# Hybrid decoder layer on one core: modulation sums packed into the first six merges, lighter paced steps, and two loads moved

## The chip, the cores and the metric

The kernel runs on one core of a Trainium2 chip. The metric is the device time of one execution in microseconds (us). TensorE (PE) multiplies matrices, VectorE (DVE) and ScalarE (ACT) work on tiles element by element, GpSimd (POOL) issues the indirect gathers and SyncE (SP) issues nearly all other DMAs. Each engine runs its own list of instructions strictly in order and waits on semaphores for the others.

## The reference, cut to what matters

Everything is float32; D = 2048, 512 tokens, 16384 experts, 16 chosen by each of 8 heads.

```python
mod = silu(c) @ w_ada + b_ada                  # 2048 -> 6 * 2048
sh1, sc1, g1, sh2, sc2, g2 = split(mod, 6)
h = rms_norm(x, norm1_w) * (1 + sc1) + sh1
q, k, v, f_logit, u, gate_s, gate_a = split(h @ w_in)
y_ssm  = half_glu(s5_mixer(u))
y_attn = fox_attention(q, k, v, f_logit)
merged = sigmoid(gate_s) * (y_ssm @ w_ssm_up) + sigmoid(gate_a) * (y_attn @ w_attn_up)
x = x + g1 * (merged @ w_out)
h2 = rms_norm(x, norm2_w) * (1 + sc2) + sh2
ids, ws = product_key_top16(h2)                # 8 heads x 16 experts for each token
a = gelu(einsum('td,ted->te', h2, expert_u[ids])) * ws
x = x + g2 * einsum('te,ted->td', a, expert_v[ids])
```

## The kernel before

A product in float32 is made of three matmuls on a high and a low part (`mm3`, lines 88 to 90). The parts of a weight come from `split`: ACT copies the high part (L94), DVE subtracts the low part (L95). Weights arrive in units of 512 KB (`wf`, issued at L100, three buffers; `whi` and `wlo` two each). In the merges and in `wout` a unit feeds 24 matmuls of 512 columns.

**The start** (0 to about 165 us) works out modulations 0 and 1 by rows on PE and DVE while it loads `w_ada`, and the setup of the S5 mixer beside it. The generator `vectors` loads `b_ada`, the norm weights and some small vectors to tiles `v`, and at its second `next` PE transposes them (L282, L286) and DVE copies them to `col1` and `col2`. Its order is written out by hand.

**The merges** (about 600 to 1098 us). `half_glu`, eight rounds of `merge` and `gates`, then `wout` (to about 1300 us) are ordered by the tile scheduler, not by hand. One round with its gates takes 11 weight units (1 of `w_ssm_up`, 2 of `w_attn_up`, 8 of `w_in`). Between rounds the kernel computes modulations 2 to 5 (`ada`): for each block of 512 columns it loads 16 tiles of 256 KB (`y`, L299), and DVE multiplies each by a column of `cond` and adds it to an accumulator (L302 for the first, L304 for the other 15). `end()` then adds over partitions with four small products against a column of ones on PE (L309, eight recorded matmuls) and DVE adds the bias (L311). There are 16 blocks. The accumulators and the `y` tiles share the pool `yp`: 28 buffers, of which the attention and S5 outputs hold 24 until the last merge. Two blocks are begun after each of the eight rounds, and the last two end after the loop.

**`wout`** makes the output projection in four quarters `q` of eight units. The input `x` is read again for the residual (`xl`, 16 small loads for each quarter, L1050, two buffers); at the end of a quarter DVE transposes a piece (L1073) and adds `g1` times the product to it (L1074), which frees the PSUM tile.

**The experts** (from about 1650 us) are ordered by hand. 320 tokens are computed densely against all experts on PE; the other 192 are gathered: `gathered` is a generator which yields after each step, first for 128 tokens (128 steps with `expert_u`, L1495, then 128 with `expert_v`, L1507), then for 64 tokens spread over 128 partitions (64 and 64), and after each group 12 light steps that scale by `g2` and add to `x2`: DVE makes diagonal tiles (`dg`, L1522), PE broadcasts them (L1526, into `A`), DVE multiplies (L1529), for the second group PE also sums the two halves (L1534), DVE adds (L1535). `pace(r)` is called at set places of the dense loops; it adds `r` to `owed` and runs one step for each whole unit. In the main loop (`value stage`, about 1895 to 3685 us) `expert_v` blocks `vf` (512 KB, L1569, three buffers) are loaded by `load_v`, split (L1577, L1580) and multiplied into 320 columns. After it stand 16 more `value` steps of 12 matmuls, each followed by one `step()`, and `finish`, which transposes the result (L1867) and stores it.

Of the kernel before, what the change touches and what calls it, by code (L numbers as in the profile page):

```python
# [7 lines left out]
F32 = mybir.dt.float32  # L8
# [9 lines left out]
P = 128  # L18
S = 512
# [18 lines left out]
VF = 3  # L38
# [11 lines left out]
NT = 6  # L50
ST = 1
S0 = 75
RS = (0, 1, 3, 4, 5, 6, 7)
SH = (0,) * 8 + (2,) * 8
TW = -(-TD // 32) * 32
# [8 lines left out]
class Builder:  # L64
# [227 lines left out]
    def ada(self, m, q, pool, bufs=None, tag="adaw"):  # L292

        nc = self.nc
        c0 = m * D + q * S
        acc = self.t(pool, [P, S], F32, "acc" if bufs else tag, bufs=1 if bufs else None)
        for i in range(KT):
            w = self.t(pool, [P, S], F32, tag, bufs=bufs)
            nc.sync.dma_start(w, self.wa[:, i, c0:c0 + S])  # L299
            col = self.cond[:, i:i + 1]  # L300
            if i == 0:
                nc.vector.tensor_scalar(acc, w, col, None, op0=ALU.mult)  # L302
            else:
                nc.vector.scalar_tensor_tensor(acc, w, col, acc, op0=ALU.mult, op1=ALU.add)  # L304

        def end():
            ps = self.t(self.ptp, [P, 4], F32, "tp")
            for c in range(4):
                nc.tensor.matmul(ps[:, c:c + 1], acc[:, c * P:(c + 1) * P], self.ones[:, 0:1], start=True, stop=True)  # L309
            s = slice(m * KT + q * 4, m * KT + q * 4 + 4)  # L310
            nc.vector.tensor_add(self.modc[:, s], ps, self.col1[:, s])  # L311

        return end
# [4 lines left out]
    def start(self, es, w_u):  # L318
# [155 lines left out]
        vectors = self.vectors(sp)  # L474
        next(vectors)
        s5 = self.s5_setup(first)
        for _ in range(S0):
            next(s5)
        next(vectors)
        nrm = norm()  # L480
        pend = iter(())
        shares = []
        for q in range(4):
            rows = [self.t(pu, [P, S], F32, "row", bufs=2) for _ in range(2)]
            accs = [None, None]
            for n in range(KT):
                m, i0 = 1 - n % 2, n // 2 * 2
                w = take("a", q, m, i0)
                for e in range(2):
                    i, src, col = i0 + e, w[:, e], self.cond[:, i0 + e:i0 + e + 1]  # L490
                    if i in PE_ROWS:
                        mm(rows[m][0:1, :], col, src, start=i == PE_ROWS[0], stop=False)
                        continue
                    if accs[m] is None:
                        accs[m] = self.t(self.apool, [P, S], F32, "a")
                        V.tensor_scalar(accs[m], src, col, None, op0=ALU.mult)
                    else:
                        V.scalar_tensor_tensor(accs[m], src, col, accs[m], op0=ALU.mult, op1=ALU.add)
                    for _ in range(ST):
                        next(s5, None)  # L500
                load()
                if q == 0:
                    if n >= NT:
                        next(nrm, None)
                else:
                    if n in RS:
                        next(pend, None)
                for _ in range(SH[n]):
                    while shares and not any(True for _ in [0] if next(shares[0], 0) is None):
                        shares.pop(0)  # L510
            for _ in pend:
                pass
            if q == 0:
                for _ in nrm:
                    pass
            pend = rest(q, accs, rows)
# [925 lines left out]
    def gathered(self, gp):  # L1442
# [44 lines left out]
        for gi, (n, _, w) in enumerate(groups):  # L1487
            if gi:
                hr = rows(0, gi)
                yield  # L1490
                yield
            av = self.t(gp, [P, n], F32, f"av{gi}")
            for s in range(n):
                g = q.pop(0)
                V.scalar_tensor_tensor(g, g, 1.0, hr, op0=ALU.mult, op1=ALU.mult, accum_out=av[:, s:s + 1])  # L1495
                used[0] += 1
                yield
            nc.scalar.activation(av, av, AF.Gelu)
            yield
            V.tensor_mul(av, av, w)  # L1500
            acc = self.t(gp, [P, D], F32, "big", bufs=1)
            for s in range(n):
                g = q.pop(0)
                if s == 0:
                    V.tensor_scalar(acc, g, av[:, 0:1], None, op0=ALU.mult)
                else:
                    V.scalar_tensor_tensor(acc, g, av[:, s:s + 1], acc, op0=ALU.mult, op1=ALU.add)  # L1507
                used[0] += 1
                yield

            m = NX if gi else P
            if gi:
                rsum = self.t(gp, [P, NX], F32, "rsum")
                V.tensor_copy(rsum, self.ident[:, 0:NX])
                for r in range(1, REP):
                    V.tensor_add(rsum, rsum, self.ident[:, r * NX:(r + 1) * NX])
            x2 = q.pop(0)
            for c4 in range(4):
                c = slice(c4 * S, (c4 + 1) * S)
                dg = self.t(self.up, [P, 4, P], F32, "ulo", bufs=4)  # L1520
                for i in range(4):
                    V.tensor_scalar(dg[:, i], self.ident, self.mcol(5, 4 * c4 + i), None, op0=ALU.mult)  # L1522
                yield
                ps = self.t(self.pA, [P, S], F32, "A", bufs=2)
                for i in range(4):
                    nc.tensor.matmul(ps[:, i * P:(i + 1) * P], self.ones, dg[:, i], start=True, stop=True)  # L1526
                if gi == 0:
                    yield
                V.tensor_mul(acc[:, c], acc[:, c], ps)  # L1529
                add = acc[:, c]  # L1530
                if gi:
                    yield
                    add = self.t(self.pA, [P, S], F32, "A", bufs=2)
                    nc.tensor.matmul(add[0:m], rsum, acc[:, c], start=True, stop=True)  # L1534
                V.tensor_add(x2[0:m, c], x2[0:m, c], add[0:m])  # L1535
                if c4 < 3:
                    yield
            nc.sync.dma_start(self.out[0, P if gi else 0:TS if gi else P], x2[0:m])
            used[0] += 1
            yield  # L1540

    def experts(self, route):
        nc, V = self.nc, self.nc.vector
# [2 lines left out]
        ND0 = self.nd0  # L1546
        up = self.up
        with ExitStack() as es:
# [146 lines left out]
            n = 0  # L1695
# [8 lines left out]
            gat = self.gathered(self.pool(es, "gath", side="right"))  # L1704

            def step(*_):
                next(gat, None)

            owed = 0.0

            def pace(r):

                nonlocal owed
                owed += r
                while owed >= 1:
                    owed -= 1
                    step()

            vp = self.pool(es, "exv")
            for i in range(VF):  # L1720
                load_v(i)
            with ExitStack() as ds:
                spread = self.spread(ds, self.rt)
                at = n
                while n == at:
                    next(tiles)
                next(spread)
                left, k = TD // 4 + 3, 4 * (ND0 - 3 - n)
                credit = 0.0

                def mid():
                    nonlocal credit
                    next(tiles)
                    credit += left / k
                    while credit > 0.5:
                        credit -= 1
                        next(spread, None)
                    if self.ahead_g:
                        self.ahead_g()
                        pace(GD)  # L1740

                self.ahead_g = None
                while n < ND0 - 3:
                    at = n
                    while n == at:
                        mid()
                    if not self.ahead_g:
                        step()
                for _ in spread:
                    pass  # L1750
            self.pep = self.pool(es, "pep", 1, PSUM)
            ep = self.pool(es, "ex")
            acc = self.t(ep, [P, KT, TD], F32, "acc")
# [139 lines left out]
    def build(self):  # L1893
        nc, tc, a, ctx = self.nc, self.tc, self.a, self.ctx
# [67 lines left out]
        for h in range(NH):  # L1962
            hi, lo = self.t(self.yp, [P, S], F32R, "y"), self.t(self.yp, [P, S], F32R, "y")
            y = self.t(self.sgp, [P, S], F32, "sg")
# [6 lines left out]
        ends = []  # L1971
        for jp in range(8):
            self.merge(jp, sgs.pop(0), ys, yh)
            if 0 < jp < 7:
                sgs.append(self.gates(jp + 1, self.sgp, "sg"))
            for end in ends:
                end()
            ends = [self.ada(2 + n % 4, n // 4, self.yp, tag="y") for n in range(2 * jp, 2 * jp + 2)]
        for end in ends:
            end()  # L1980
        r2.close()
        n2 = ctx.enter_context(ExitStack())
        wo = ctx.enter_context(ExitStack())
# [64 lines left out]
```

## Time and profile before

| | |
|---|---|
| three runs | 3755.02, 3755.24, 3746.28 us; median 3755.02 |
| profiled execution | 3749.76 us, its span 3748.0 us |
| mean granted TensorE clock | 0.985 |
| busy share of the span | PE 96%, DVE 81%, ACT 35%, POOL 20% |

The span runs from the first to the last recorded instruction; the execution's own time is 1.76 us longer. Times of rows are counted from the span's start. A granted clock of 1.00 is 2.4 GHz, 0.50 is 1.2 GHz.

### The profile page before, as it was taken

How to read it: one execution, taken by the hardware profiler on the slowest of the kernel's cores; microseconds unless marked ns; L12 is line 12 of the kernel's file. 1: busy time of each engine (PE TensorE's matmuls, PEld its weight loads, DVE VectorE, ACT ScalarE, POOL GpSimd, SP SyncE). 2: the span in 40 equal slices, each digit the busy share in tenths (PEclk: the TensorE clock that was granted, in tenths of full speed). 3: DMA queues.
4: the chain of work that ended last, by engine and by line, in shares of the span. 5: the costliest groups of instructions: out<-in, count | busy, mean ns of one | idle time of the engine just before them, and what ended most of it. 6: DMA issues, size and time to landing. Idle time of an engine off the chain costs nothing. (4 is left out here: it accounts for less than half of the span.)

```text
span 3748.0 us, 58747 instructions
## 1 busy us (share of the span) xinstructions
PE 3600.1 (96%) x22974; PEld 3326.5 (89%) x22974; DVE 3043.6 (81%) x4731; ACT 1320.4 (35%) x2273; POOL 743.5 (20%) x520
## 2 busy tenths in 40 slices
PE   6999999999997989999989999999999999999998
PEld 2698886888875889998989999999999999999997
DVE  6578886555575478869979999999999978999997
ACT  2334454222221253345644333333333333333332
POOL 0000000000000043425621222222222212222221
PEclk8999999999998999999999999999999999999999
DMA  8732224667766543248999999999999969999996
GB/s 284 238 86 77 82 77 127 189 197 213 219 220 181 143 134 104 81 142 316 338 343 311 328 367 373 365 357 371 375 368 366 367 252 347 377 373 353 368 371 212
DMA packets 471689, 973.95 MB, mean 260 GB/s; under 512 B 67402, under 2 KB 337908, under 8 KB 404724
## 3 DMA queue, kind: packets, MB, share of 16 engines
q1 hardware_dynamic: 416116, 567.53, 46.4%
q0 software_dynamic: 55296, 402.68, 27.8%
q8 instruction: 180, 2.95, 0.3%
q14 instruction: 97, 0.79, 0.1%
HBM read 930.31 MB, written 39.71 MB: 259 GB/s over the span
## 5 line engine op out<-in xcount | busy, mean ns | idle before, releaser
L88 PE MATMUL A<-hi,uhi 128*128 128x320 f32 x2048 | 658.1, 321 | 0.0
L88 PE MATMUL V<-ghi,vhi 128*128 128x320 f32 x2048 | 651.1, 318 | 2.0 <-ACT acc L1689 1.5
L89 PE MATMUL V<-glo,vhi 128*128 128x320 f32 x2048 | 632.5, 309 | 3.0 <-DVE glo L1669 3.0
L90 PE MATMUL V<-ghi,vlo 128*128 128x320 f32 x2048 | 632.6, 309 | 2.4 <-DVE vlo L1580 2.2
L90 PE MATMUL A<-hi,ulo 128*128 128x320 f32 x2048 | 633.1, 309 | 0.0
L89 PE MATMUL A<-lo,uhi 128*128 128x320 f32 x2048 | 632.7, 309 | 0.0
L1601 ACT CAST uhi<-tp 128x512 fp32r<-128x512 f32 x512 | 300.9, 588 | 605.8 <-PE tp L1597 595.7
L1495 DVE SCALAR_TENSOR_TENSOR g<-g,big 128x2048 f32<-128x2048 f32 x192 | 438.0, 2283 | 23.1 <-DMA big<-hx 15.4
L1507 DVE SCALAR_TENSOR_TENSOR big<-g,av,big 128x2048 f32<-128x2048 f32 x190 | 445.5, 2345 | 10.0 <-DMA g<-in_peer_v_dram,ids 7.9
L89 PEld LDWEIGHTS V<-glo,vhi 128*128 128x128 f32 x2048 | 385.5, 188 | 4.4 <-DVE glo L1669 4.2
L88 PEld LDWEIGHTS V<-ghi,vhi 128*128 128x128 f32 x2048 | 385.1, 188 | 4.6 <-issue 1.9
L90 PEld LDWEIGHTS V<-ghi,vlo 128*128 128x128 f32 x2048 | 384.5, 188 | 3.1 <-DVE vlo L1580 3.1
L89 PEld LDWEIGHTS A<-lo,uhi 128*128 128x128 f32 x2048 | 386.6, 189 | 0.0
L88 PEld LDWEIGHTS A<-hi,uhi 128*128 128x128 f32 x2048 | 386.2, 189 | 0.0
L90 PEld LDWEIGHTS A<-hi,ulo 128*128 128x128 f32 x2048 | 385.3, 188 | 0.0
L1580 DVE TENSOR_TENSOR vlo<-vf,vhi 128x1024 fp32r<-128x1024 f32 x248 | 302.4, 1220 | 30.7 <-ACT vhi L1577 30.5
L1577 ACT CAST vhi<-vf 128x1024 fp32r<-128x1024 f32 x248 | 259.4, 1046 | 186.4 <-PE V L89 135.0
L304 DVE SCALAR_TENSOR_TENSOR y<-y,cond,y 128x512 f32<-128x512 f32 x240 | 187.2, 780 | 168.4 <-DMA y<-in_w_ada_dram 165.2
L1597 PE MATMUL tp<-ident,uf 128*128 128x128 f32 x2048 | 308.1, 273 | 11.7 <-DMA uf<-in_peer_u_dram 6.3
L1608 DVE TENSOR_TENSOR ulo<-tp,uhi 128x512 fp32r<-128x512 f32 x412 | 280.3, 680 | 36.5 <-ACT uhi L1601 29.2
L94 ACT CAST whi<-wf 128x1024 fp32r<-128x1024 f32 x146 | 153.9, 1055 | 439.7 <-PE mx L89 228.1
L1597 PEld LDWEIGHTS tp<-ident,uf 128*128 128x128 f32 x2048 | 254.9, 141 | 24.4 <-DVE wT L1659 6.5
(475 smaller groups left out, 7308.7 us busy)
## 6 DMA issues: line engine op xcount, KB each, us to landing
uf<-in_peer_u_dram SPq DMA_DIRECT2D x128, 1024.0 KB
vf<-in_peer_v_dram SPq DMA_DIRECT2D x248, 512.0 KB
y<-in_w_ada_dram SPq DMA_DIRECT2D x256, 256.0 KB
wf<-in_w_in_dram SPq DMA_DIRECT2D x116, 512.0 KB
wd<-ev SPq DMA_DIRECT2D x40, 512.0 KB
wt<-wd SPq DMA_DIRECT2D x128, 160.0 KB
adaw<-in_w_ada_dram SPq DMA_DIRECT2D x32, 512.0 KB
wf<-in_w_ada_dram SPq DMA_DIRECT2D x32, 512.0 KB
```

Of the source, the lines that this page charges most:

```text
L88: mm(ps, lhi, rhi, start=start, stop=False)
L89: mm(ps, lhi, rlo, start=False, stop=False)
L90: mm(ps, llo, rhi, start=False, stop=stop)
L94: nc.scalar.copy(hi, src)
L304: nc.vector.scalar_tensor_tensor(acc, w, col, acc, op0=ALU.mult, op1=ALU.add)
L1495: V.scalar_tensor_tensor(g, g, 1.0, hr, op0=ALU.mult, op1=ALU.mult, accum_out=av[:, s:s + 1])
L1507: V.scalar_tensor_tensor(acc, g, av[:, s:s + 1], acc, op0=ALU.mult, op1=ALU.add)
L1577: nc.scalar.copy(vhi, vf)
L1580: V.tensor_sub(vlo, vf, vhi.bitcast(F32))
L1597: mm(tp[:, k], ufs[i][:, (4 * c + k) * P:(4 * c + k + 1) * P], self.ident, is_transpose=True, start=k == 0, stop=False, skip_group_check=True)
L1601: nc.scalar.copy(hi, tp)
L1608: late.append(on_pe if i < ND0 - 3 else lambda: V.tensor_sub(lo, tp, hi.bitcast(F32)))
```

## The change

1. `AD` gives how many modulation blocks are begun after each merge: three after merges 0 to 3, two after merges 4 and 5, none after 6 and 7 (before: two after each). The accumulator is taken from the pool `a` (20 buffers) instead of `yp`.
2. The second `next(vectors)` of the start moves from before the loop to its ninth round.
3. The 12 light steps of a gathered group yield 0.35 and the two after the reload of `hr` 0.5; `pace` takes off what the step returns, instead of 1.
4. The first three `vf` tiles are loaded in three rounds of the deferred stage (n = 22, 23, 24) instead of together where the pool `exv` opens.

```diff
+AD = (0, 3, 6, 9, 12, 14, 16, 16, 16)
...
-        acc = self.t(pool, [P, S], F32, "acc" if bufs else tag, bufs=1 if bufs else None)
+        acc = self.t(self.apool, [P, S], F32, "a")
...
-        next(vectors)
         nrm = norm()
...
                 if q == 0:
+                    if n == 8:
+                        next(vectors)
...
                 hr = rows(0, gi)
-                yield
-                yield
+                yield 0.5
+                yield 0.5
...
                     V.tensor_scalar(dg[:, i], self.ident, self.mcol(5, 4 * c4 + i), None, op0=ALU.mult)
-                yield
+                yield 0.35
                 ps = self.t(self.pA, [P, S], F32, "A", bufs=2)
...
             def step(*_):
-                next(gat, None)
+                return next(gat, None) or 1.0
...
                 while owed >= 1:
-                    owed -= 1
-                    step()
+                    owed -= step()
...
-            for i in range(VF):
-                load_v(i)
...
                     at = n
+                    if 0 <= n - ND0 + 3 + VF < VF:
+                        load_v(n - ND0 + 3 + VF)
...
-            ends = [self.ada(2 + n % 4, n // 4, self.yp, tag="y") for n in range(2 * jp, 2 * jp + 2)]
-        for end in ends:
-            end()
+            ends = [self.ada(2 + n % 4, n // 4, self.yp, tag="y") for n in range(AD[jp], AD[jp + 1])]
```

The other four `yield`s of the light steps change in the same way. In the changed file the lines named here stand one or two further down (L299 is L300, L309 is L310, L1050 is L1052, L1526 is L1528, L1534 is L1536).

**Where the modulations end.** In the list of PE before, one of the 16 closing products stands in the last merge and four stand in `wout`, whose PSUM tiles are `mx` and `mm` and whose activations are `h`. Two places of `wout`, the second of them in its first quarter's last units:

```order
L88 MATMUL mx_10034<-h_9938,whi_10068 128x512
L89 MATMUL mx_10034<-h_9939,whi_10068 128x512
L309 MATMUL tp_9803<-ones_69,y_9603 128x1 x4
L90 MATMUL mx_10034<-h_9938,wlo_10069 128x512
...
L90 MATMUL mx_10322<-h_9942,wlo_10357 128x512
L309 MATMUL tp_9913<-ones_69,y_9815 128x1 x4
L309 MATMUL tp_9919<-ones_69,y_9864 128x1 x4
L88 MATMUL mm_10321<-h_9930,whi_10326 128x512
```

Of the change, the last two of the 16 stand between the gates of round 7 (`mm_9686`) and the last merge (`mx_9823`):

```order
L91 MATMUL mm_9686<-h_1113,wlo_9780 128x512
L310 MATMUL tp_9811<-ones_69,a_9359 128x1 x4
L310 MATMUL tp_9817<-ones_69,a_9408 128x1 x4
L89 MATMUL mx_9823<-y_6408,whi_9827 128x512
```

All 16 of them now come before the last merge.

**SP's queue.** In the list of SP before, the end of the modulation loads, inside `wout`, is this (16 `y` loads stand between two of its weight units, of which the last two are shown, and then the first `xl` loads):

```order
L299 DMA y_9861<-in_w_ada_dram 128x512
L100 DMA wf_10466<-in_w_out_dram 128x2x512
...
L299 DMA y_9907<-in_w_ada_dram 128x512
L299 DMA y_9910<-in_w_ada_dram 128x512
L1050 DMA xl_9998<-in_x_dram 32x16x32 x16
L1050 DMA xl_10015<-in_x_dram 32x16x32 x4
L100 DMA wf_10496<-in_w_out_dram 128x2x512
```

Of the change, the last `y` loads and the first `xl` loads:

```order
L101 DMA wf_9621<-in_w_in_dram 128x4x256
L300 DMA y_9451<-in_w_ada_dram 128x512
L300 DMA y_9454<-in_w_ada_dram 128x512
L101 DMA wf_9651<-in_w_in_dram 128x4x256
...
L101 DMA wf_10126<-in_w_out_dram 128x2x512
L1052 DMA xl_9998<-in_x_dram 32x16x32 x2
L101 DMA wf_10156<-in_w_out_dram 128x2x512
L1052 DMA xl_9998<-in_x_dram 32x16x32 x2
```

The last `y` load now stands before the last five units of the gates, and ahead of it four or five `y` loads stand between two weight units instead of two or three. The `xl` loads of the first quarter go between its units from the fifth on; the last two of them stand behind the second unit of the second quarter.

**The light steps.** In the list of PE before, the light steps of the second group stand after the value stage, between the last `value` products (`V`) and `finish` (`tp`):

```order
L1526 MATMUL A_37234<-ulo_37209,ones_69 128x128 x4
L1867 MATMUL tp_37240<-ident_64,acc_17677 128x128 x4
...
L90 MATMUL V_37264<-ghi_37095,vlo_37162 128x320
L1534 MATMUL A_37280<-big_34152,rsum_37206 64x512
L88 MATMUL V_37264<-ghi_36631,vhi_37161 128x320
```

Of the change, they stand in the last two of the 128 rounds of the value stage; the first of the four:

```order
L1599 MATMUL tp_36958<-ident_64,uf_36636 128x128 x4
L1528 MATMUL A_36974<-ulo_36969,ones_69 128x128 x4
L1536 MATMUL A_36980<-big_33709,rsum_36966 64x512
L89 MATMUL V_36941<-ghi_35968,vhi_36793 128x320
```

The broadcast (L1528) and the sum (L1536), which needs DVE's product of what L1528 gives, follow each other without another matmul between them in three of the four; no light step is left after the value stage.

## Rows read from the trace of the kernel before

**Rows 1.** The page: the span, and TensorE's busy time, share and instructions.
```profile
span 3748.0 us, 58747 instructions
...
PE 3600.1 (96%) x22974; PEld 3326.5 (89%) x22974; DVE 3043.6 (81%) x4731; ACT 1320.4 (35%) x2273; POOL 743.5 (20%) x520
```

**Rows 2.** Waits of PE, 1050 to 1330 us: total, times, longest, in us.
```profile
PE tp L309 <- DVE y L304: 21.4, 5, 13.1
PE mm L88 <- DVE a L1074: 10.5, 1, 10.5
```

**Rows 3.** Windows: PE, PEld, DVE, ACT, POOL busy (instructions), clock, DMA share, GB/s.
```profile
1050.00:1100.00 50.00, 47.62 (x206) 38.27 (x205) 36.11 (x50) 19.38 (x27) 1.66 (x1) 0.97 0.69 214
1100.00:1150.00 50.00, 45.64 (x190) 36.49 (x189) 33.60 (x43) 7.90 (x9) 2.21 (x1) 0.93 0.70 234
1150.00:1200.00 50.00, 24.82 (x106) 19.70 (x105) 29.59 (x41) 6.96 (x15) 0.00 (x0) 0.73 0.63 181
1200.00:1250.00 50.00, 50.00 (x217) 40.23 (x217) 18.57 (x21) 11.79 (x13) 0.00 (x0) 1.00 0.55 127
```

**Rows 4.** Timeline of SP's queue and DVE, 1155 to 1190 us.
```profile
1155.70 11.07 SPq L299 DMA_DIRECT2D y<-in_w_ada_dram  x16
...
1162.54 11.78 DVE L304 SCALAR_TENSOR_TENSOR y<-y,cond,y 128x512 f32<-128x512 f32 x15 [0.27 <-DMA y<-in_w_ada_dram]
...
1176.33 10.43 SPq L1050 DMA_DIRECT2D xl<-in_x_dram  x20
...
1185.25 0.71 DVE L1073 STREAM_TRANSPOSE a<-xl 128x512 f32<-128x512 f32 x1 [8.75 <-DMA xl<-in_x_dram]
```

**Rows 5.** Windows of the merges, of `wout`'s first part and of the y loads.
```profile
850.00:900.00 50.00, 50.00 (x224) 40.55 (x223) 28.04 (x36) 11.64 (x13) 0.00 (x0) 1.00 0.69 211
1085.00:1105.00 20.00, 20.00 (x87) 16.10 (x86) 16.25 (x19) 5.25 (x6) 3.87 (x2) 1.00 0.80 265
1160.00:1165.00 5.00, 1.02 (x8) 0.97 (x8) 3.19 (x7) 0.00 (x0) 0.00 (x0) 0.85 1.04 393
```

**Rows 6.** Timeline of SP's queue and DVE, 856 to 865 us.
```profile
856.28 4.84 SPq L299 DMA_DIRECT2D y<-in_w_ada_dram  x3
...
860.01 0.75 DVE L304 SCALAR_TENSOR_TENSOR y<-y,cond,y 128x512 f32<-128x512 f32 x1 [2.97 <-DMA y<-in_w_ada_dram]
860.68 1.22 DVE L95 TENSOR_TENSOR wlo<-wf,whi 128x1024 fp32r<-128x1024 f32 x1
863.53 0.75 DVE L304 SCALAR_TENSOR_TENSOR y<-y,cond,y 128x512 f32<-128x512 f32 x1 [0.96 <-DMA y<-in_w_ada_dram]
```

**Rows 7.** Timeline of PE and SP's queue in the start.
```profile
19.96 0.45 PE L282 MATMUL tp<-ident,v 128*128 128x128 f32 x1 [12.31 <-DMA v<-in_norm_w_dram]
...
22.89 2.32 SPq L356 DMA_DIRECT2D adaw<-in_w_ada_dram  x2
```

**Rows 8.** Windows of the loop's end and of what follows it.
```profile
3600.00:3650.00 50.00, 50.00 (x356) 49.96 (x355) 47.72 (x47) 16.91 (x26) 14.77 (x11) 1.00 0.98 366
3685.00:3748.00 63.00, 44.71 (x271) 38.19 (x271) 39.59 (x62) 12.74 (x19) 1.68 (x1) 0.89 0.52 168
```

**Rows 9.** Groups of PE, 3685 to 3748 us: busy, mean ns, idle before.
```profile
L1867 PE MATMUL tp<-ident,acc 128*128 128x128 f32 (+1 forms) x48 | 8.3, 316 | 1.1 <-ACT ulo L1869 0.8
L1526 PE MATMUL A<-ulo,ones 128*128 128x128 f32 x32 | 5.3, 319 | 10.5 <-DVE ulo L1522 10.5
L1534 PE MATMUL A<-big,rsum 128*64 128x512 f32 x8 | 4.3, 618 | 0.0
```

**Rows 10.** Timeline of PE after 3685 us, its longest wait there.
```profile
3705.07 2.08 PE L1526 MATMUL A<-ulo,ones 128*128 128x128 f32 x8 [10.05 <-DVE ulo L1522]
```

**Rows 11.** Timeline of DVE at the second group's first step.
```profile
3109.91 2.29 DVE L1495 SCALAR_TENSOR_TENSOR g<-g,big 128x2048 f32<-128x2048 f32 x1 [6.59 <-DMA big<-hx]
```

**Rows 12.** Timeline of SP's queue where the pool `exv` opens.
```profile
1658.89 1.48 SPq L1569 DMA_DIRECT2D vf<-in_peer_v_dram  x3
```

**Rows 13.** Window ahead of the value stage.
```profile
1750.00:1850.00 100.00, 99.06 (x759) 96.00 (x758) 100.00 (x139) 60.33 (x132) 63.30 (x35) 1.00 0.97 347
```

More of the change, by code (lines that the diff above doesn't have):

```diff
@@ L1527, in gathered @@
                 if gi == 0:
-                    yield
+                    yield 0.35
                 V.tensor_mul(acc[:, c], acc[:, c], ps)
@@ L1531, in gathered @@
                 if gi:
-                    yield
+                    yield 0.35
                     add = self.t(self.pA, [P, S], F32, "A", bufs=2)
@@ L1536, in gathered @@
                 if c4 < 3:
-                    yield
+                    yield 0.35
             nc.sync.dma_start(self.out[0, P if gi else 0:TS if gi else P], x2[0:m])
             used[0] += 1
-            yield
+            yield 0.35
     def experts(self, route):
```

## The prediction

> **What bounds the kernel now.** The page comes first: PE is busy for 3600.1 of the 3748.0 us [rows 1]. So nearly every stage is set by PE's own work, and time can come back only where PE stands still, runs at the lower of its two clocks, or does work that could be spared. The change spares no matmul; it must gain in PE's 148 idle us. The next view is the list of PE's waits in the stretch where the modulations end. Five closing products L309 wait there for DVE's accumulations L304, 21.4 us in all, 13.1 the longest, and one matmul of `wout` waits 10.5 us for a PSUM tile that DVE frees at L1074 [rows 2]: 31.9 us. The windows say the same in another way: from 1050 to 1200 us PE began 206 + 190 + 106 = 502 matmuls, while the undisturbed 50 us behind them hold 217, so 651 would have fitted [rows 3]. The 149 missing ones at 50/217 = 0.230 us are 34.3 us. The 2.4 us above the waits fit the granted clock, 0.97, 0.93 and 0.73 in these windows: after each stop some matmuls ran at 1.2 GHz.
>
> The timeline shows the mechanism. At 1155.70 SP issues 16 `y` loads in a row, DVE works through 15 of them in 11.78 us, and only at 1176.33, behind them all, come the 20 `xl` loads; the first transpose of `xl` on DVE waits for them until 1185.25 [rows 4]. The modulations are late, and they make the residual late.
>
> **Part 1, the modulations, removed work.** All 16 closings now stand before the last merge and all `y` loads before its gates, so `wout` holds neither. Both waits of [rows 2] and the half clock behind them have no cause left there. I take 34 us (31.9 by the waits, 34.3 by the windows). What remains possible in `wout` is that the first quarter's last two `xl` loads, which now stand behind a unit of the second quarter, come late: one wait of 0 to 4 us (4 is an estimate, less than half of the 10.5). I put 1.
>
> **Part 1, added load.** The same 256 `y` tiles are pressed into six rounds, 48 in each of the first four. A round is 11 units of 24 matmuls at 0.230 us, 61 us, in which PE never stops now: 50.00 of 50, at 211 GB/s and a DMA share of 0.69 [rows 5]. After it, a round must move 48 × 0.262 + 11 × 0.524 = 18.3 MB, 301 GB/s. The nearest stretch is `wout`'s first part, 265 GB/s with PE at 20.00 of 20; a stretch of loads alone reached 393 [rows 5]. DVE must do 48 × 0.75 + 11 × 1.22 = 49 us of these 61 [rows 6], beside some 3 us of small products. So neither is full, but the slack falls from near a half to a sixth.
>
> What decides is the number of buffers. A tile must turn over every 61/48 = 1.27 us. The accumulators' move leaves four buffers for weights instead of two. The rows show a load used 3.7 us after its issue (856.28 to 860.01), and another 2.4 us after the last issue of its group (861.12 to 863.53), and 0.75 us of use [rows 6]: 3.2 to 4.5 us for a turn. With two buffers that is 1.6 to 2.2 us for a tile (today's need is 61/32 = 1.9), with four 0.8 to 1.1, under 1.27. I take it as hidden under PE's matmuls. Without that cover: `wlo` (L95) stands behind the `y` steps on DVE, PE has only one split unit in hand, and each 0.1 us beyond 1.27 costs 4.8 us in each of four rounds. Sum of part 1: −34 + 1 = −33, from −36 to −15.
>
> **Part 2, the vectors.** PE's first transpose waits 12.31 us for the small loads `v`, until 19.96, and the row products, whose weights came long before, stand behind it; their buffers come free late and the next weight load issues at 22.89 [rows 7]. Now two rows of L492 stand ahead. Its release point becomes the end of the `v` issues on SP, about 20 us, where PE's wait for those loads ended. So up to 22.89 − 19.96 = 2.9 us; after it the transposes, no longer late, cost PE nothing new. I take −3, bounds −5 and 0 (0 if later loads, not the first ones, set the start's end).
>
> **Part 3, the light steps.** In the value loop PE has no gap: 50.00 of 50, 356 matmuls, 0.140 us each [rows 8]. What follows takes 63 us, of which PE works 44.71. In it are the second group's light steps, 5.3 + 4.3 us at L1526 and L1534, and a wait of 10.5 us at L1526 [rows 9]; 10.05 of it is one wait, until 3705.07, for a diagonal tile that DVE can only make after its last gathered steps [rows 10]. Since a light step now costs a third, the gather runs some 16 steps ahead (12 × 0.65 in each group and 2 × 0.5 at the reload) and its last step falls into the loop's last round. What is left after the loop: 16 values × 12 matmuls × 0.140 = 27 us, the transposes 8.3 us [rows 9], and around them a start and an end in which PE has nothing: today 63 − 44.71 − 10.5 = 8 us. That is about 43.5; gain 19.
>
> It is not all gain. The 9.6 us of light products (8.5 at the full clock, an estimate from the fastest of four) go into a loop where PE is full, and cost their whole time. And the light steps now follow each other so closely that PE meets DVE's products with nothing between: a diagonal takes DVE 0.9 us, a product 0.7, behind what DVE has queued, perhaps a step of 2.3. For the second group's four columns I put 5 us (2 to 10), for the first group's, where two broadcasts stand right behind their diagonals, 2 (0 to 4). The reload of `hr` cost DVE 6.59 us of waiting with no wait of PE [rows 11]; with less between issue and use DVE waits perhaps a microsecond longer, 0 to 2 on PE, and I put 0.5. Sum: −19 + 8.5 + 5 + 2 + 0.5 = −3, bounds −9 and +6.
>
> **Part 4, the first `vf`.** They were issued at 1658.89 in 1.48 us, ahead of other loads but in a light place [rows 12]. Their first use is the first value, after 1895. Now 1.57 MB go into the stretch ahead of it, which at 0.97 of the DMA engines moves 347 GB/s, while DVE is busy 100 of 100 and PE 99.06 [rows 13]. At 347 GB/s they are worth 4.5 us if everything behind them is late by as much, 0 if DVE, which is full itself, hides that. PE has lost less than 1 us in that 100, so I stay near the low end, +1. The gain of leaving the old place is nothing: no PE wait stands there for these loads.
>
> One rule speaks against this part: the Trainium skill, page "DMA: Bandwidth & Descriptors", section Specifications, gives about 358 GB/s as the limit of the HBM for a core. By it the stretch at 347 would be at its ceiling, the part would cost its whole 1.57 MB/358 GB/s = 4.4 us, and the sum would be 3.4 us higher. The window with 393 GB/s [rows 5] lies above that figure, so the measurement decides here, and the sum stays.
>
> **Sum.** −33 − 3 − 3 + 1 = −38 on the profiled execution's own 3749.8 us: 3711.8. Two of the three runs shown lie 5 us above that execution, one 3.5 below it, so the same change seen from their median would be 3717; I forecast 3712.
>
> **Rivals.**
>
> *Slower: the loads become the bound of the merges.* If at 301 GB/s a `y` load lands later than today, DVE waits, `wlo` is late and PE stops at the first matmul of a unit. With four buffers the need of 1.27 holds up to a landing of 4 × 1.27 − 0.75 = 4.3 us; the longest read above is 3.7. At a landing of 5.1 us a tile takes 1.47, a round 70.5 instead of 61, and 4 × 9.5 = 38 us eat the whole gain; from there on the kernel is slower. With a tile at 1.66, as if the second pair of buffers did nothing, it is 4 × 18.7 = 75 us, 3787. For it: only 15% of slack on both DVE and DMA. Against it: 265 GB/s under full PE with no wait, and 0.785 us a tile when 15 buffers stood ready [rows 4]. Chance 0.06.
>
> *The closings wait in the merges.* The 16 products move to places of the scheduler's choice, right behind a round's last unit. Four of the five waits of today share 21.4 − 13.1 = 8.3 us, 2.1 each. If PE waits 3 us in each of the six rounds, 18 us come back and the time is 3730. For it: the tighter DVE. Against: the closings of today's merges stop nothing in a window at 50.00 of 50 [rows 5]. Chance 0.17.
>
> *The light steps cost more than they give.* Stalls at their upper bounds, and part 4 at its own: 14 us and 4.5 instead of 7 and 1, so 3723. It lies near the forecast and shares its chance.
>
> *The change does not do what it says.* Modulations end earlier, but `wout` then waits for `xl` or for its weights as long as before; only the 21.4 us or less go, and light steps and loads give 15 back: about 3745, no change that can be told. Chance 0.06.
>
> **How the numbers follow.** The forecast case, 3694 to 3726, has 0.64. The closings' case has 0.17 (3726 to 3740), the undone change 0.06, the slower case 0.06, and a larger gain, below 3694, 0.07 (tail or start better than their terms). Leaving out the slower case, the undone one above 3742 and most of the larger gain, the range is 3692 to 3742. About 0.3%, 11 us, can be told from no change: faster than 3744 holds the first two cases, the larger gain and a part of the undone one, 0.89; within it 0.05; slower 0.06.
>
> **What would show it.** Right: no wait of PE at L310 and none at L1074 from 1050 to 1330, the window after the last merge at a clock of 1.00, merges still at 50 of 50 with some 300 GB/s, the stretch after the value loop about 44 us, and no L1526-like row in it. Wrong: waits of PE for `wlo` between 660 and 1050 (the loads are the bound), waits at L310 there (the closings), a start that ends no earlier, or PE idle in the last rounds of the value loop by over 10 us.

## The result, and the profile after

The changed kernel takes 3711.19 us (median of four runs, 3704.29 to 3714.58), before 3751.53 us (four runs): ratio 0.9891, 95% interval 0.9869 to 0.9914. The forecast was 3712, its range 3692 to 3742. Its profiled execution took 3714.58 us and has a span of 3712.8 us, 35.2 less than that of before. TensorE's busy time is on balance the same as in [rows 1]; idle time went. The page's first lines:

```profile
span 3712.8 us, 58759 instructions
...
PE 3599.9 (97%) x22974; PEld 3324.2 (90%) x22974; DVE 3046.1 (82%) x4731; ACT 1319.7 (36%) x2273; POOL 734.6 (20%) x520
```

The two traces can be laid beside each other at instructions that both have. Each number is how much earlier (−) or later (+) than in the trace of before the instruction starts, in us; the rows below the first two are runs of the next section.

| | end of the start (ACT copies u) | last merge's last product (DVE, L1026) | last residual of `wout` (DVE, L1074) | first `value` sum (DVE, L1691) | last product with the experts' weights in the value loop (DVE, L1849) | span |
|---|---|---|---|---|---|---|
| before, us | 159.5 | 1100.4 | 1321.0 | 1959.8 | 3684.0 | 3748.0 |
| the change | −2.1 | +14.8 | −23.7 | −24.8 | −12.7 | −35.2 |
| the change again | −4.0 | +12.6 | −25.8 | −28.6 | −15.5 | −38.0 |
| part 1 alone | −0.7 | +11.1 | −27.4 | −27.0 | −26.8 | −27.1 |
| part 3 alone | +4.7 | −0.2 | +0.7 | −0.9 | +11.9 | −10.6 |
| parts 2 and 4 alone | −2.0 | −6.7 | −6.3 | −5.1 | −4.5 | −1.9 |
| early start | −2.9 | +1.5 | −36.9 | −36.5 | −23.0 | −45.1 |
| one closing tile | −0.1 | +5.5 | −33.0 | −33.7 | −20.6 | −43.2 |
| pace instead | −3.8 | +11.5 | −27.0 | −29.6 | −20.1 | −42.7 |
| early, one tile, pace | +2.7 | +4.9 | −33.6 | −33.5 | −24.0 | −46.4 |

Read along the second row: the start gives 2.1, the merges take 16.9, `wout` gives 38.5, the experts' preparation 1.1, the value loop takes 12.1, and what follows it gives 22.5. One execution's stage can differ by some us from another's: part 3 alone, which has the start of before, ended it 4.7 us later. The large steps repeat; the start's 2.1 is within that scatter. For the merges the scatter is least from the first product with the gates in pool `sg` (L1023) to the last (L1026): there the change and the four other traces that have its merges took 9.9 to 14.1 us more than the trace of before, the two others with the merges of before 3.4 and 3.5 us less, and the five with the edits of early start or of one tile 0.6 to 3.1 us more.

**`wout`** is what was forecast. The windows that answer to [rows 3], at the full clock and without a pause; the missing matmuls are back:

```profile
1050.00:1100.00 50.00, 50.00 (x223) 40.54 (x222) 23.46 (x29) 19.93 (x27) 3.97 (x2) 1.00 0.31 94
1100.00:1150.00 50.00, 50.00 (x216) 40.16 (x215) 15.81 (x17) 10.61 (x11) 3.49 (x2) 1.00 0.47 116
1150.00:1200.00 50.00, 50.00 (x219) 40.02 (x218) 18.48 (x22) 12.38 (x21) 0.00 (x0) 1.00 0.55 135
```

**The merges** now have waits at `wlo` and at the closings of every full round. Before, PE waited there at one closing only, in the last merge (PE's waits of before from 600 to 1105 us: total, times, longest):

```profile
PE tp L309 <- DVE y L304: 2.4, 1, 2.4
```

The same list of the change, of which the 4.0 and the 0.7 stood there before too:

```profile
PE mm L91 <- DVE wlo L96: 4.8, 5, 2.0
PE tp L310 <- DVE modc L312: 4.2, 4, 2.3
PE mm L89 <- issue: 4.0, 1, 4.0
PE mm L90 <- DVE y L96: 0.7, 1, 0.7
```

The timeline of PE at the closings of a round: two run at once, the third waits until DVE has read one of two PSUM tiles, `tp`:

```profile
756.72 1.84 PE L310 MATMUL tp<-ones,a 128*128 128x1 f32 x16
759.58 1.05 PE L310 MATMUL tp<-ones,a 128*128 128x1 f32 x8 [0.45 <-DVE modc L312]
...
823.73 1.84 PE L310 MATMUL tp<-ones,a 128*128 128x1 f32 x16
826.73 1.05 PE L310 MATMUL tp<-ones,a 128*128 128x1 f32 x8 [0.59 <-DVE modc L312]
...
889.85 1.84 PE L310 MATMUL tp<-ones,a 128*128 128x1 f32 x16
894.52 1.86 PE L310 MATMUL tp<-ones,a 128*128 128x1 f32 x8 [2.26 <-DVE modc L312]
```

From one closing pair to the next the rounds with three blocks take 823.73 − 756.72 = 67.0 us, then 66.1 and 72.6, where the forecast had 61. SP's queue and windows of the merges show the rest. No modulation runs from 640 to 693 us (DMA at 99 GB/s, before at 225): SP fills the four buffers at 633.41 us, and the next `y` load waits until the second merge has freed an accumulator's buffer of pool `a` (timeline of SP's queue):

```profile
633.41 1.92 SPq L300 DMA_DIRECT2D y<-in_w_ada_dram  x4
...
693.85 0.34 SPq L300 DMA_DIRECT2D y<-in_w_ada_dram  x1
```

Then the load is at 0.85 of the DMA engines, and the short stops leave the clock below 1.00:

```profile
640.00:693.00 53.00, 53.00 (x227) 42.58 (x227) 13.36 (x13) 12.15 (x14) 1.29 (x1) 1.00 0.33 99
850.00:900.00 50.00, 47.26 (x203) 37.98 (x202) 35.32 (x47) 10.31 (x12) 0.00 (x0) 0.95 0.85 274
950.00:1000.00 50.00, 47.14 (x200) 37.79 (x199) 36.53 (x48) 8.45 (x9) 3.02 (x2) 0.93 0.78 257
```

**The end.** The window after the value loop, which answers to the second of [rows 8], is 42 us long instead of 63, and PE's waits from 3500 us on have no 10 us at the broadcast (L1526 in [rows 9, 10], here L1528) any more:

```profile
3671.00:3713.00 42.00, 35.37 (x244) 33.43 (x242) 23.53 (x34) 13.09 (x19) 0.00 (x0) 0.97 0.59 188
```

```profile
PE A L1536 <- DVE big L1531: 2.5, 3, 0.9
PE tp L1868 <- DVE acc L1883: 1.3, 1, 1.3
PE tp L1868 <- ACT ulo L1870: 1.0, 4, 0.3
PE A L1528 <- DVE ulo L1524: 0.5, 1, 0.5
```

**The start.** PE's 12.3 us of waiting for the vectors [rows 7] is gone, and a wait for the next weights stands in its place. That load is issued at 20.31 us instead of 22.89, still behind the small loads of the vectors. PE's waits for these weights grew from 11.0 to 21.2 us over the whole start (timelines of SP's queue and of PE):

```profile
20.31 0.91 SPq L357 DMA_DIRECT2D adaw<-in_w_ada_dram  x2
...
23.80 5.43 PE L492 MATMUL row<-adaw,cond 128*1 128x512 f32 x8 [6.52 <-DMA adaw<-in_w_ada_dram]
```

### The profile page after: what moved, and what is told of

The parts are those of the page before. It is cut to its first block, busy times and chain, and to the rows that moved or that the text cites. A ratio compares the mean times of both kernels' runs of the same rounds, so it can differ in the third digit from the quotient of the medians.

```text
span 3712.8 us, 58759 instructions
## 1 busy us (share of the span) xinstructions
PE 3599.9 (97%) x22974; PEld 3324.2 (90%) x22974; DVE 3046.1 (82%) x4731; ACT 1319.7 (36%) x2273; POOL 734.6 (20%) x520
## 4 chain that ended last, share of the span: by engine, by line
PE 77%; DVE 10%; DMA 8%; issue 2%; ACT 2%; SPq 1%; DVEq 0%; ACTq 0%
PE A L89 7%; PE A L91 7%; PE V L90 7%; PE A L90 7%; PE V L89 7%; PE V L91 7%; PE tp L1599 5%; DMA y<-in_w_ada_dram 5%; PE mm L90 2%; PE mm L89 2%; PE mm L91 2%; PE mm L202 2%; PE mm L204 2%; PE mm L203 2%; DVE a L305 2%
## 5 line engine op out<-in xcount | busy, mean ns | idle before, releaser
L1509 DVE SCALAR_TENSOR_TENSOR big<-g,av,big 128x2048 f32<-128x2048 f32 x190 | 446.0, 2347 | 11.5 <-DMA g<-in_peer_v_dram,ids 7.0
L1599 PE MATMUL tp<-ident,uf 128*128 128x128 f32 x2048 | 308.0, 273 | 12.3 <-DVE ulo L1610 9.2
L96 DVE TENSOR_TENSOR wlo<-wf,whi 128x1024 fp32r<-128x1024 f32 x114 | 145.3, 1275 | 179.3 <-ACT whi L95 157.4
```

Of the source, the lines that this page charges most:

```text
L96: return (lo_eng or nc.vector).tensor_sub(lo, src, hi.bitcast(F32))
L1599: mm(tp[:, k], ufs[i][:, (4 * c + k) * P:(4 * c + k + 1) * P], self.ident, is_transpose=True, start=k == 0, stop=False, skip_group_check=True)
```

## The experiments

**The parts alone.** Before, with one part of the change each (the diff's lines of that part and no others).

> Kernel before with part 1 alone (three modulation blocks after merges 0 to 3, accumulators from pool a). By the traces of before and of the change, the stretch from the first weight unit of the merges to the end of wout became 21.6 us shorter: some 38 us less in wout, some 17 more in the merges. If the four parts add up, this kernel is 20 to 23 us faster than before, and its PE waits on wlo and on the closing products in the merges are those of the change (9 to 10 us). Rival, the prediction's own term: 33 us faster, the loss in the merges then being caused by another part. A second rival: under 10 us, if the wout gain needs the earlier start of part 2.

3724.72 us, ratio 0.994 (0.9923 to 0.9957), where before took 3748.41 beside it: 22.5 us less by the ratio, 23.7 by the medians. By the trace its merges end 11.1 us later than before and its `wout` 27.4 us earlier. PE's waits in the merges, 2.8 us on `wlo` and 4.1 at the closings, are 6.9 us and not the 9 to 10 expected.

> Kernel before with part 3 alone (light steps count 0.35). By the two traces the value loop became 12 us longer and what follows it 22.5 us shorter. Theory: the light steps' matmuls cost their whole time in the loop (8.5 us) plus about 3 us of waits, and the tail loses them and the waits for DVE's last gathered steps; 10 us faster than before, the tail about 40 to 41 us. Rival, the prediction's own term: 3 us faster, tail 44 us, stalls of 7 us in the loop.

3736.96 us, ratio 0.9968 (0.9956 to 0.9981), 12 us less by the ratio, 11.5 by the medians; by the trace 12.8 us into the loop and 22.5 out of the tail.

> Kernel before with parts 2 and 4 alone (vectors later, first vf loads later). Theory: the start ends 2.1 us earlier, because PE's wait for the vectors (12.3 us) is replaced by a wait for the next weight load, which SP still issues only behind the small vector loads; the vf loads cost 0 to 1 us. Sum -1 to -2 us, not to be told from no change by its time; read from the trace. Rival: vf loads cost 4.5 us in the full stretch, so 2 us slower.

3746.62 us, ratio 0.9997 (0.9987 to 1.0007): no change that can be told. The stretch from `wout` to the first value sum, in which part 4 would cost, takes 1.2 us more than before here and 1.1 less in the change; the two runs above, without part 4, have 0.5 more and 1.5 less. So its 4.5 us are refuted. The three ratios sum to −0.95%, the change has −1.09%: the parts add up within the intervals, and part 1 is two thirds.

**Two buffers.** What decided for the merges in the prediction was the number of weight buffers.

```diff
-        self.yp = self.pool(r2, "yp", 28)
+        self.yp = self.pool(r2, "yp", 26)
```

> The changed kernel with yp of 26 buffers instead of 28, so that two are left for the weights of the modulations instead of four. If the number of buffers sets how fast the tiles turn over (1.6 to 2.2 us a tile with two, against a need of 1.27 or 1.3), each of the four rounds with 48 tiles takes 77 to 106 us instead of 67 to 70, and the kernel is 40 to 130 us slower than the change, so slower than before. Rival: DVE's own load (52 of 61 us) or SP's queue sets the pace, then two buffers do about as well as four and the time is within 10 us of the change.

3821.72 us, ratio 1.0198 (1.0178 to 1.0217): slower than before, some 110 us slower than the change. SP's queue issues the loads of one stretch in 37.09/21 = 1.77 us each, in the 1.6 to 2.2 that [rows 6] gave for two buffers, and the wait falls on the closings (timeline of SP's queue, then PE's waits from 600 to 1300 us):

```profile
840.49 37.09 SPq L300 DMA_DIRECT2D y<-in_w_ada_dram  x21
```

```profile
PE tp L310 <- DVE a L305: 97.8, 10, 26.5
```

So the denser schedule needs the four buffers that moving the accumulators leaves it. The Trainium skill, page "DMA: Bandwidth & Descriptors", section "Anatomy of one DMA", gives a load that GpSimd issues about 2.0 us and its bytes at 436 GB/s: 2.6 us for one of these tiles, so with 0.75 us of use an estimate of 1.68 us for two buffers. The trace comes near it, although SP issues these loads. Those of this stretch (830 to 880 us) land 2.8 us after their issue (median), and (2.8 + 0.75)/2 is the 1.77 measured.

**Where the merges lose.** Three edits of the changed kernel. Early start, with `NS` = 2:

```diff
-AD = (0, 3, 6, 9, 12, 14, 16, 16, 16)
+AD = (0, 4, 7, 9, 12, 14, 16, 16, 16)
...
-        acc = self.t(self.apool, [P, S], F32, "a")
+        acc = self.t(*(acc or (self.apool, [P, S], F32, "a")))
...
-            ends = [self.ada(2 + n % 4, n // 4, self.yp, tag="y") for n in range(AD[jp], AD[jp + 1])]
+            ends = [self.ada(2 + n % 4, n // 4, self.yp, tag="y", acc=(self.sgp, [P, S], F32, "sg") if n < NS else None) for n in range(AD[jp], AD[jp + 1])]
```

> The changed kernel, but four blocks are begun after the first merge (4, 3, 2, 3, 2, 2 instead of 3, 3, 3, 3, 2, 2), and the accumulators of the first two come from the pool sg, which is free then. In the changed kernel no modulation runs from about 640 to 693 us, because the accumulators wait for a buffer of pool a that only the second merge frees; DMA moves 108 GB/s there. Theory: the rounds of the merges are long because 48 tiles are pressed into each; with blocks already in the empty stretch a third of that goes away, PE's waits on wlo and on the third closing fall, 5 to 9 us faster than the change. Rival: the waits come from the scheduler's placing of closings and splits, not from the load of the rounds; then the time is that of the change.

3704.15 us, ratio 0.9882 (0.9865 to 0.9898); the interval overlaps that of the change, so its time alone does not tell it apart. Read from the trace the merges end 1.5 us later than before instead of 14.8. The empty stretch is filled, the later windows are at the full clock, and PE's waits are down (windows, then waits from 600 to 1105 us):

```profile
640.00:693.00 53.00, 52.85 (x226) 42.20 (x225) 33.85 (x42) 11.79 (x14) 1.29 (x1) 1.00 0.78 253
850.00:900.00 50.00, 49.86 (x222) 40.01 (x221) 36.85 (x50) 10.60 (x12) 0.00 (x0) 1.00 0.88 287
```

```profile
PE mm L92 <- DVE wlo L97: 1.8, 3, 1.2
PE tp L311 <- DVE modc L313: 0.3, 1, 0.3
```

This edit does two things at once: it fills the empty stretch, and it leaves three rounds with three blocks or more instead of four.

One PSUM tile for a round's closings (all products first, then DVE's additions):

```diff
-        def end():
-            ps = self.t(self.ptp, [P, 4], F32, "tp")
+        def end(ps):
...
-            nc.vector.tensor_add(self.modc[:, s], ps, self.col1[:, s])
+            return lambda: nc.vector.tensor_add(self.modc[:, s], ps, self.col1[:, s])
...
+    def closes(self, ends):
+        if ends:
+            ps = self.t(self.ptp, [P, 4 * len(ends)], F32, "tp")
+            for add in [end(ps[:, 4 * i:4 * i + 4]) for i, end in enumerate(ends)]:
+                add()
...
-            for end in ends:
-                end()
+            self.closes(ends)
```

> The changed kernel, but all closing products of a round write slices of one PSUM tile, and DVE adds the bias afterwards; in the change the third closing of a round waits for DVE to have read one of two PSUM tiles, 4.2 us in all. Theory: these 4.2 us and the half clock behind them go, 4 to 6 us faster than the change; waits on wlo (4.8 us) stay. Rival: the third closing then waits for its own accumulation, DVE being behind, and nothing is gained.

3706.63 us, ratio 0.9891 (0.9874 to 0.9907): by its time not to be told from the change. By the trace the merges end at +5.5. The wait for `modc` is gone, one of 0.8 us for an accumulation is new, 3.5 us on `wlo` stay. The stretch from 640 to 693 us is still empty, yet the later window is at the full clock:

```profile
640.00:693.00 53.00, 53.00 (x228) 42.57 (x227) 13.67 (x13) 12.04 (x14) 0.00 (x0) 1.00 0.31 102
850.00:900.00 50.00, 50.00 (x228) 40.69 (x227) 37.45 (x51) 11.51 (x13) 0.00 (x0) 1.00 0.89 287
```

The vectors' loads further back:

```diff
-        next(vectors)
         s5 = self.s5_setup(first)
...
-                    if n == 8:
+                    if n in (3, 10):
```

> The changed kernel, but the loads of the vectors are issued in the start loop's fourth round, behind five loads of weights and input, and their transposes stand in its eleventh round. In the change PE waits 6.5 us for the first new weight load, which SP issues at 20.31 us, behind 3.6 us of small vector loads. Theory: that load is issued at 16.7 us and the start ends 3 to 4 us earlier. Rival: the start is set by its later loads, then it ends when it does in the change, and the gain of 2.1 us of part 2 did not come from the first loads either.

3709.89 us, ratio 0.9899 (0.9883 to 0.9916); the first weight load is issued at 16.57 us, as expected, but the start ends at −3.6, only 1.5 us earlier than in the change. PE's wait for weights fell from 21.2 to 17.8 us in all, but its transposes, now in the eleventh round, wait 3.6 us for the vectors. No gain that can be told.

> The three edits of the other runs of this call together: early modulations, one closing tile, vectors behind. If each gives what its theory says and they add up, 12 to 18 us faster than the change, some 3693 to 3700 us where the change takes 3711. If the merges keep waits on wlo, or the start does not move, 4 to 8 us.

3704.79 us, ratio 0.9894 (0.9876 to 0.9912): by the medians the smaller of the two expectations, by the ratio not to be told from the change. The start ended at +0.1, so the edit of the vectors gave nothing; the merges at +3.5.

**Cheap steps or an early end.** Without part 3, but with the loop's pace raised so that the second group ends at the same row:

```diff
-GF = 0.85
+GF = 0.89
```

> The changed kernel itself, unaltered, so that the next three can be compared with it on one chip: 0.988 to 0.990 of before.

3712.71 us, ratio 0.9909 (0.9895 to 0.9924).

> The changed kernel without its part 3 (light steps count 1 again), but with the pace of the main loop raised from 0.85 to 0.89, so that the last light step of the second group stands at the same row of PE's list as in the change (19884), with its broadcasts and sums 13 or more rows apart from each other. Theory: what part 3 is worth comes from the gather's end falling inside the loop, not from light steps being cheap: within 4 us of the change, the tail 40 to 41 us, the loop longer by the light matmuls (8.5 us) but without the 3 us of waits at the broadcasts and sums. Rival: DVE and DMA have no room for heavy steps 5% closer together, then PE waits for DVE in the loop and the kernel is over 10 us slower than the change.

3707.28 us, ratio 0.9901 (0.9886 to 0.9916), beside 0.9909 of the change on the same chip: the same. From the first value sum to the loop's last weight product it takes 9.5 us more than before; the change took 12.1 and 13.1. The 2.5 and 0.5 us of waits at the light steps are not in its rows, and what follows the loop gives 22.6 us, as with part 3. That the steps count a third is not what gives the time; that the gather ends inside the loop is.

> The changed kernel with early_start and one_closing_tile together, without the edit of the vectors. By the traces of those two runs the merges ended 13 and 9 us earlier than in the change; both work on the same waits, so theory: the merges end 12 to 16 us earlier than in the change, PE waits under 3 us there, and the kernel is 6 to 14 us faster than the change. Rival: the executions of one kernel differ by as much in the merges and the time is that of the change.

3705.31 us, ratio 0.9894 (0.9879 to 0.9909); merges end at +2.4, that is 10 us earlier than in the change on this chip and not the 12 to 16 expected; PE still waits 3.3 us on `wlo`. Its interval and the change's overlap.

> early_one_tile with the edit of pace_instead. If both theories hold, as fast as early_one_tile or up to 4 us faster: 0.985 to 0.988 of before. Rival: slower than the change, if the raised pace costs PE waits in the loop.

3697.69 us, ratio 0.9866 (0.985 to 0.9881), against 0.9909 (0.9895 to 0.9924) of the change: the intervals do not meet, 15 us less by the medians. This is the fastest kernel here, 7.6 us below `early_one_tile` by the medians where up to 4 were expected. By the traces its merges, counted as above, are 13 us and its loop 4 us shorter than those of the change on this chip; its start was 6.7 us later in that execution.

## Why the prediction was right, and where it was not

**`wout`: right.** The waits at L309 and L1074 are gone with the half clock behind them. The step gave 38.5 us instead of 34. Of [rows 2] 29.5 us lie in `wout` proper (the first of the five waits, 2.4 us, is in the last merge); four closings' own work, about 1 us each, left it as well and moved into the merges; the rest, about 5 us, is the clock, of which I had counted half. The reckoning by windows hid this: its 502 matmuls hold 48 one-column records of closings, each counted as a whole matmul. Without them, 264 of the 434 that would have fitted began from 1100 to 1200 us, and the 170 missing at 0.230 us are 39.2 us. The 1 us for a late `xl` did not appear.

**The merges: the step that failed.** "I take it as hidden under PE's matmuls" did not hold: the merges and the start's rest took 16.9 us more. Of these 4 are the moved closings, whose work the forecast had put at nothing here, 4.8 the waits on `wlo`, 4.2 the waits of the third closing, less the 2.4 that went. Of what is left, about 6, the clock is 5: from the start's end to the last merge its mean is 0.988 over 957.8 us, and was 0.993 over 940.9, which is 11.9 us of lost clock against 6.8. Both signs that I had named for a wrong term, waits on `wlo` and at L310, are there.

The reckoning per tile held where it was tried, at 1.77 us with two buffers. What it left out is that only two PSUM tiles serve the three closings of a round. `one_closing_tile` shows this: it takes away that wait alone, and the merges, counted as above, take 3.1 us more than before instead of 14.1. The same count is 9.9 to 13.8 in the four other traces with the merges of the change, so the cut is clear of the scatter, though not in the run's time. The reckoning also left out that the loads stand still until the second merge frees an accumulator. What that costs by itself is not shown. `one_closing_tile` has the same empty stretch and loses little. `early_start` fills the stretch, has three full rounds instead of four, and its third closings wait 0.3 us in all; its merges take 2.7 us more than before. By these traces the late start cost mostly through the same wait. Together the two edits give little more than either. The waits on `wlo` are the smaller part: 1.6 to 4.8 us in the five traces with the merges of the change, 1.4 to 3.5 in those with the edits. The rival of the closings named the place, and its 18 us come near the 16.9, but not the cause: it expected DVE to be late with the accumulation. Part 1 as a whole was −21.6 us between the start's end and that of `wout`, −26.7 in the trace of its own run and −22.5 by that run's ratio; the forecast was −33, its bounds −36 to −15.

**The vectors: not settled.** The 2.1 us of the trace lie near the 3 that were forecast, but starts of the same code scatter by more, and neither the run of parts 2 and 4 nor the one with later loads moved the time. The three traces with the start of before end it at 0, −0.7 and +4.7 us, the nine with that of the change at −4.0 to +2.7, −1.7 in the mean. The means are 3 us apart, as forecast, but the two groups overlap. What the rows show is that one wait took another's place.

**The light steps: right in kind, mis-sized.** Loop +12.1 against a forecast of 16, since the stalls were 3.0 us and not 7; tail −22.5 against −19, since 41.5 us were left and not 43.5, of 64.0 where I had counted 63. So −10.4 instead of −3, and its own run had −12 by the ratio. `pace_instead` confirms the work term: without stalls the loop is longer by 9.5 us, of which 8.5 were the forecast for the matmuls.

**The first `vf`: nothing** was paid, +1 was forecast. The Trainium skill, page "DMA: Bandwidth & Descriptors", section Specifications, would have made it 4.4 us through a limit of about 358 GB/s; the run of parts 2 and 4 does not show it, and the start of the changed kernel moves 405 GB/s for 4 us:

```profile
24.00:28.00 4.00, 4.00 (x6) 0.60 (x5) 0.00 (x0) 0.00 (x0) 0.00 (x0) 0.56 1.01 405
```

**The sum** met the result because two errors went opposite ways: 11 us too much in part 1, 7 too little in part 3. That is luck, and so is the agreement to 1 us: the forecast started from the profiled execution, which went down by 35.2 us and not 38, to 3714.58, while the medians lie 40.3 us apart.

## What to carry to other kernels

When work is packed into a stretch that has slack on average, look for what frees its first buffer and for the smallest pool that several pieces now share: here an accumulator's pool delayed the start by some 50 us, and two PSUM tiles served three closings, a wait whose removal gave the merges 7 to 11 us by the traces. Paced background work should end inside the loop that hides it; whether by cheaper steps or by a faster pace made no difference in the time of a run, though the faster pace left the loop about 3 us shorter in both traces that have it. A total that comes out right says nothing of its terms; lay the two traces beside each other at common instructions.

## What the runs showed of the hardware

Short stops of PE cost more than their length. In the window from 850 to 900 us of the changed kernel PE waited 2.74 us and began 203 matmuls; in `one_closing_tile` the same window has no wait and 228, and both hold 24 one-column records of closings. The 25 missing at 0.230 us are 5.8 us, so each microsecond of these waits cost about 2.1. The 3 us beyond the waits are about what the clock lost: it was granted at 0.95 over the 50 us instead of 1.00.

In the start both kernels ran their first products behind a long stop at about half pace. In the change the granted clock is 0.56 from 24 to 28 us, most of it the lower level of 1.2 GHz, behind 6.5 us of waiting (shown above). Before, behind 12.3 us [rows 7], the first four row products took 3.57 us, and later eight took 3.60, which is the pace of 1.2 GHz and then of 2.4:

```profile
21.22 3.57 PE L492 MATMUL row<-adaw,cond 128*1 128x512 f32 x4
...
29.14 3.60 PE L492 MATMUL row<-adaw,cond 128*1 128x512 f32 x8
```

A window from 24 to 28 us reads a clock of 1.00 in the trace of before, but that trace has no record of the clock ahead of 26.8 us; there the pace of the products decides.
